# Dealing the depthwise convolution of a streaming encoder layer by channel tile: prompt tiles on POOL, VectorE and TensorE

## The chip, the cores and the metric

One core of a Trainium2 chip runs the kernel. The metric is the device time of one execution in microseconds (us); lower is better. The engines are TensorE (PE, with PEld for its weight loads), VectorE (DVE), ScalarE (ACT), GpSimd (POOL) and SyncE (SP), whose queue issues nearly all DMAs. Each engine runs its instructions strictly in the order of its own stream, and waits at an instruction whose inputs are not there.

## What is computed

The reference is one step of a two-layer streaming encoder: layer 0 is a Conformer convolution module, layer 1 is attention, and each is followed by a SwiGLU feed-forward block. The change lies in the convolution module:

```python
def conv_module(h, hist, g, w_pw1, b_pw1, w_dw, b_dw, ln_g, ln_b, w_pw2, b_pw2):
    a, gate = jnp.split(rms_norm(h, g) @ w_pw1 + b_pw1, 2, axis=-1)
    glu = a * jax.nn.sigmoid(gate)
    full = jnp.concatenate([hist.astype(glu.dtype), glu], axis=1)
    y = lax.conv_general_dilated(
        full, w_dw[:, None, :].astype(full.dtype), window_strides=(1,), padding="VALID",
        dimension_numbers=("NWC", "WIO", "NWC"), feature_group_count=D_MODEL) + b_dw
    y = jax.nn.silu(layer_norm(y, ln_g, ln_b))
    return h + y @ w_pw2 + b_pw2, full[:, -CONV_HIST:]
```

There are 1024 channels and two groups of frames: a prompt of 512 frames (one stream) and a sample group of 8 streams with 16 frames each. The depthwise convolution has 31 taps: every channel is convolved with its own 31 weights. All is float32.

## The kernel before, in words

**Layout.** Channels lie on the 128 partitions, in eight channel tiles (0 to 7). The 640 columns are 128 sample frames and then 512 prompt frames. They are cut into two column groups of 320 (`NH`): group 0 is the sample and the first 192 prompt frames, group 1 is the rest. `gall` holds the convolution's input per channel tile: `gs`, eight sample segments of 30 history and 16 new frames (368 columns), then `gp`, the prompt with its padding (544 columns).

**First projection (GLU).** `glu(c, g, ...)` (L552) computes tile c for group g: two PSUM tiles `mm` (value and gate), 24 matmuls of 320 columns each (three per k-tile, since a float32 product is made of high and low parts: L159 to L161). ACT evacuates both (L562 `t1`, L565 `t2`), and DVE multiplies them into `gall` (L569, L575). The pool `mm` has four PSUM buffers. A tile's weights come by `wsplit` (L118): a 1 MB load into `raw`, then ACT writes the rounded high part `whi` (L139) and DVE or POOL the low part `wlo` (L143). The table `PL1` says how many quarters of `wlo` POOL makes: 4 of 4 for tiles 2 to 7.

**Depthwise convolution, on DVE.** `conv` (L580) takes one or two tiles of the sample group: 31 instructions of 128x128 per tile, each multiplying a shifted window by one tap's weight and adding it to an accumulator in PSUM (L588, L591). Tiles 0 to 5 of the sample group are done so.

**Depthwise convolution, on PE.** `conv_load` (L596) lets POOL build block-diagonal weights `w4` (L598) and copies the tile's row of `gall` to a scratch `sc` in DRAM (L603). `conv_shift` (L606) reads it back in four DMAs, one per shift of 0 to 3 frames, each to 32 partitions (L609): `x4p` for the prompt, `x4s` for the sample. `conv_pe` (L613) then runs 32 matmuls of 32 output channels (L622; each shows as two in the profile), and ACT moves the result to `y` (L628). All eight prompt tiles and the sample of tiles 6 and 7 are done so. A prompt tile is one pass of 512 columns (step `p`), or is cut in 192 columns for group 0 (`A`) and 320 for group 1 (`B`).

**The rest of the module.** `conv_ln` (L631) normalizes over all 1024 channels of a group: sums over the tiles by PE with a column of 1/D (L194), spread to all partitions (L206), subtraction, squares, sums again, and silu. It needs `y` of all eight tiles. `pw2` (L651) is the second projection, with matmuls again on L159 to L161.

**What sets the order.** The string `PLAN` (L61) lists the steps: `a`, `b` are tile 0's and 1's GLU for the two groups, `cN` loads and computes the GLU of tile N, `lN` is `conv_load` and the prompt's `conv_shift`, `pN`, `AN`, `BN`, `SN` are PE convolutions (`S` is the sample group and loads its own `x4s`), `dMN` is the DVE convolution of two tiles, `n` is the norm, `w` the second projection. The tile framework's scheduler then lays every engine's stream: it keeps to the plan's order as a priority and puts a later instruction ahead where it takes an earlier one to be not ready; steps in `tc.high_priority` come sooner. On the chip the streams are fixed.

Of the kernel before, what the change touches and what calls it, by code (L numbers as in the profile page):

```python
# [8 lines left out]
F32 = mybir.dt.float32  # L9
# [6 lines left out]
P = 128  # L16
D = 1024
KT = D // P
# [23 lines left out]
HP = 2000  # L42
CUT, LCUT = 8, 6
PO = {2: 0, 4: 1}
PL1 = (0, 2, 4, 4, 4, 4, 4, 4)
PL2 = (2, 2)
SQ = 'aaaaaaaa'
C01 = 4
# [20 lines left out]
def tile_trunk(ctx, tc, xT, vecs, hist, w_pw1, w_pw2, w_in0, w_out0, w_in1, w_out1,  # L69
# [181 lines left out]
    def rms_late(g, gain, engs=SQ, cut=CUT):  # L251
        n = gr[g][1]
        xh, xl = new_xs(g)
        for k in range(KT):
            src = hp(g, k)
            if gain is not None:
                t = tp.tile([P, 384], F32, tag="n1", name=nm("n1"), bufs=NB1)
                nc.vector.tensor_scalar(out=t[:, :n], in0=src, scalar1=col(gain, k),
                                        scalar2=None, op0=ALU.mult)
                src = t[:, :n]  # L260
            xsplit(src, xh[:, k, :], xl[:, k, :])
        rt = cst.tile([P, 4], F32, tag=f"rt{g}", name=nm("rt"))
        bc, _ = rstd_bc([hp(g, k) for k in range(KT)], n, engs, cut, rt)
        b = xp.tile([P, n], F32, tag=f"bc{g}", name=nm("bc"))
        nc.scalar.activation(out=b, in_=bc, func=AF.Copy)
        return xh, xl, b, rt
# [308 lines left out]
            nc.vector.scalar_tensor_tensor(out=gp[:, c, o:o + n - ns], in0=t[:, ns:n], scalar=1.0,  # L575
                                           in1=a[:, ns:n], op0=ALU.add, op1=ALU.mult)

    def conv(cs):
        n = NB * SB
        st = w2t()  # L580
        sts = [st[:, i * 512:i * 512 + n] for i in range(len(cs))]
        for j in range(W):
            for i, c in enumerate(cs):
                src = gs[:, c, :, j:j + SB]
                dst = sts[i].rearrange("p (s w) -> p s w", w=SB)
                wj = dcol(V_DW + c * W + j)
                if j == 0:
                    nc.vector.tensor_scalar(out=dst, in0=src, scalar1=wj, scalar2=col(V_BDW, c),  # L588
                                            op0=ALU.mult, op1=ALU.add)
                else:  # L590
                    nc.vector.scalar_tensor_tensor(out=dst, in0=src, scalar=wj, in1=dst,  # L591
                                                   op0=ALU.mult, op1=ALU.add)
        for i, c in enumerate(cs):
            nc.scalar.activation(out=y[0][:, c, 0:n], in_=sts[i], func=AF.Copy)

    def conv_load(c):  # L596
        w4 = cp.tile([P, 32, 32], F32, tag="w4", name=nm("w4"), bufs=3)
# [5 lines left out]
        nc.sync.dma_start(sc, gall[:, c, :])  # L603
        return w4, sc

    def conv_shift(sc, tag, a, n, bufs):  # L606
        x4 = cp.tile([P, 4, n], F32, tag=tag, name=nm(tag), bufs=bufs)
        for s in range(4):
            nc.sync.dma_start(x4[32 * s:32 * s + 32],  # L609
                              sc[:, a + s:a + s + n].rearrange("(q p) w -> p q w", q=4))  # L610
        return x4

    def conv_pe(c, w4, x4, a, n):  # L613
        pt = mmt()
        for tg in range(8):
            for q in range(4):
                if a < 0:
                    mv = x4[:, q, :].rearrange("p (s w) -> p s w", w=SEG)
                    mv = mv[:, :, 4 * tg:4 * tg + SB]
                else:  # L620
                    mv = x4[:, q, a + 4 * tg:a + 4 * tg + n]
                nc.tensor.matmul(pt[32 * q:32 * q + 32, 0:n], w4[:, 4 * tg + q, :], mv,  # L622
                                 start=(tg == 0), stop=(tg == 7))
        o = 0 if a < 0 else NB * SB + a
        for g in range(2):
            u, v = max(o, g * NH), min(o + n, g * NH + NH)
            if u < v:
                nc.scalar.activation(out=y[g][:, c, u - g * NH:v - g * NH], in_=pt[:, u - o:v - o],  # L628
                                     func=AF.Identity, bias=col(V_BDW, c))

    def conv_ln(g):  # L631
        n = gr[g][1]
# [33 lines left out]
    zs, pws, x4s, scs = {}, {0: w00, 1: w01}, {}, {}  # L666

    def step(op, arg):
        cs = [int(c) for c in arg]
        c = cs[0] if cs else 0  # L670
        if op == "a":
            glu(c, 0, *pws[c])
        elif op == "b":
            glu(c, 1, *pws[c])
        elif op == "c":
            w = wsplit(w_pw1[c], 16, P, pool=PL1[c])
            load_hist(c, c + 1)
            glu(c, 0, *w)
            glu(c, 1, *w)
        elif op == "y":  # L680
            load_x(1)
        elif op == "x":
            xs[1] = rms(1, V_NCONV, SSQ1, 8)
        elif op == "l":
            scs[c] = conv_load(c)
            x4s[c] = conv_shift(scs[c][1], "x4p", NSC, NPC - 4, 3)
        elif op == "d":
            conv(cs)
        elif op == "S":
            conv_pe(c, scs[c][0], conv_shift(scs[c][1], "x4s", 0, NSC, 1), -1, NB * SB)  # L690
        elif op in "pAB":
            a, n = {"p": (0, T), "A": (0, NH - NB * SB), "B": (NH - NB * SB, NH)}[op]
            conv_pe(c, scs[c][0], x4s[c], a, n)
# [450 lines left out]
```

## Time and profile before

| what | value |
|---|---|
| median of three runs | 1612.81 us (1612.3 to 1614.66) |
| the profiled execution | 1610.26 us, its span 1608.3 us |
| mean granted TensorE clock over the span | 0.972 of full speed |
| PE busy over the span | 1521.2 us, 95% |
| DVE, ACT, POOL busy | 967.9 us (60%), 635.4 us (40%), 193.4 us (12%) |
| convolution stage: tile 2's GLU to the first matmul of `pw2` | from 62.60 to 241.14 us |

The profile is one execution, taken by the hardware profiler. A row of the timeline has the start, the time until the last instruction of the row ends, engine, line, operation, tiles written and read, and count; in brackets stands the idle time ahead of it and what ended that. "SPq" rows are DMA issues on SP's queue, not the transfers. A row of the windows has the busy time and count of each engine in a stretch, then the granted TensorE clock, the mean busy share of the 16 DMA engines, and GB/s. Consecutive PE instructions overlap, so a row's first instruction starts before the previous row's last has ended.

### The profile page before, as it was taken

How to read it: one execution, taken by the hardware profiler on the slowest of the kernel's cores; microseconds unless marked ns; L12 is line 12 of the kernel's file. 1: busy time of each engine (PE TensorE's matmuls, PEld its weight loads, DVE VectorE, ACT ScalarE, POOL GpSimd, SP SyncE). 2: the span in 40 equal slices, each digit the busy share in tenths (PEclk: the TensorE clock that was granted, in tenths of full speed). 3: DMA queues.
4: the chain of work that ended last, by engine and by line, in shares of the span. 5: the costliest groups of instructions: out<-in, count | busy, mean ns of one | idle time of the engine just before them, and what ended most of it. 6: DMA issues, size and time to landing. Idle time of an engine off the chain costs nothing.

```text
span 1608.3 us, 27216 instructions
## 1 busy us (share of the span) xinstructions
PE 1521.2 (95%) x11220; PEld 1426.8 (89%) x11220; DVE 967.9 (60%) x1984; ACT 635.4 (40%) x1233; POOL 193.4 (12%) x209
## 2 busy tenths in 40 slices
PE   4899789899999999999899899997999999999997
PEld 4877669889999999999888688894899999999996
DVE  7943014696566666557366766665585576666555
ACT  3312224544334244245445444454354244244243
POOL 5233303300000000002322111110100000000001
PEclk9999978899999999999999999999899999999998
DMA  6444702311312312222455445554102223213211
GB/s 216 132 131 132 196 14 79 122 36 58 111 69 76 108 62 77 99 79 79 150 175 179 165 141 170 163 172 133 65 27 79 79 80 92 88 58 105 79 54 66
DMA packets 56924, 168.78 MB, mean 105 GB/s; under 512 B 10081, under 2 KB 23009, under 8 KB 48097
## 3 DMA queue, kind: packets, MB, share of 16 engines
q1 hardware_dynamic: 56512, 166.75, 32.5%
q8 instruction: 88, 1.44, 0.4%
q10 hardware_dynamic: 288, 0.31, 0.1%
q14 instruction: 36, 0.29, 0.1%
HBM read 153.80 MB, written 13.23 MB: 104 GB/s over the span
## 4 chain that ended last, share of the span: by engine, by line
PE 89%; DVE 4%; DMA 3%; issue 2%; ACT 1%; POOL 1%; POOLq 0%; DVEq 0%; ACTq 0%; SPq 0%
PE mm L351 34%; PE mm L159 15%; PE mm L161 14%; PE mm L160 14%; PE mm L622 3%; DMA cache<-in_ck 1%; PE w L941 1%; PE am L926 1%; PE am L972 1%; PE am L909 1%; PE w L885 1%; DMA x4s<-sc 1%; PE w L886 1%; PE w L206 1%; PE w L194 1%
## 5 line engine op out<-in xcount | busy, mean ns | idle before, releaser
L351 PE MATMUL mm<-XH,wlo 128*128 128x320 f32 x736 | 229.1, 312 | 1.6 <-DVE wlo L309 1.6
L351 PE MATMUL mm<-XH,whi 128*128 128x320 f32 x736 | 227.3, 311 | 0.0
L351 PE MATMUL mm<-XL,whi 128*128 128x320 f32 x736 | 225.6, 309 | 0.0
L159 PE MATMUL mm<-xh,whi 128*128 128x320 f32 (+2 forms) x640 | 204.2, 321 | 6.2 <-ACT xh L148 5.6
L160 PE MATMUL mm<-xh,wlo 128*128 128x320 f32 (+2 forms) x640 | 203.1, 318 | 2.8 <-POOL wlo L143 2.5
L161 PE MATMUL mm<-xl,whi 128*128 128x320 f32 (+2 forms) x640 | 197.7, 316 | 0.0
L160 PE MATMUL mm<-hid,wlo 128*128 128x320 f32 (+2 forms) x560 | 171.9, 308 | 0.0
L161 PE MATMUL mm<-hid,whi 128*128 128x320 f32 (+2 forms) x560 | 169.4, 308 | 0.0
L159 PE MATMUL mm<-hid,whi 128*128 128x320 f32 (+2 forms) x560 | 167.7, 308 | 0.0
L308 ACT ACTIVATE whi<-raw 128x1536 fp32r<-128x1536 f32 (+2 forms) x90 | 101.0, 1149 | 121.7 <-PE mm L161 87.6
L309 DVE TENSOR_TENSOR wlo<-raw,whi 128x1536 fp32r<-128x1536 f32 (+2 forms) x90 | 118.7, 1341 | 40.5 <-ACT whi L308 40.4
L351 PEld LDWEIGHTS mm<-XH,wlo 128*128 128x128 f32 x736 | 139.2, 189 | 2.9 <-DVE wlo L309 2.9
L351 PEld LDWEIGHTS mm<-XH,whi 128*128 128x128 f32 x736 | 138.6, 189 | 0.0
L351 PEld LDWEIGHTS mm<-XL,whi 128*128 128x128 f32 x736 | 138.3, 189 | 0.0
L159 PEld LDWEIGHTS mm<-xh,whi 128*128 128x128 f32 x640 | 124.5, 195 | 12.3 <-ACT xh L148 6.6
L160 PEld LDWEIGHTS mm<-xh,wlo 128*128 128x128 f32 x640 | 124.8, 195 | 4.1 <-POOL wlo L143 2.7
L161 PEld LDWEIGHTS mm<-xl,whi 128*128 128x128 f32 x640 | 122.2, 193 | 1.6 <-issue 1.4
L351 PE MATMUL mm<-XH,vhi 128*128 128x320 f32 x368 | 115.0, 313 | 0.3 <-ACT XH L435 0.3
L351 PE MATMUL mm<-XL,vhi 128*128 128x320 f32 x368 | 114.5, 312 | 0.9 <-DVE XL L436 0.8
L351 PE MATMUL mm<-XH,vlo 128*128 128x320 f32 x368 | 114.8, 312 | 0.0
L160 PEld LDWEIGHTS mm<-hid,wlo 128*128 128x128 f32 x560 | 105.1, 188 | 0.0
L161 PEld LDWEIGHTS mm<-hid,whi 128*128 128x128 f32 x560 | 104.6, 188 | 0.0
(199 smaller groups left out, 3316.5 us busy)
## 6 DMA issues: line engine op xcount, KB each, us to landing
raw<-in_w_in SPq DMA_DIRECT2D x38, 1024.0 KB
cache<-in_ck SPq DMA_DIRECT2D x32, 512.0 KB
cache<-in_cv SPq DMA_DIRECT2D x32, 512.0 KB
raw<-in_w_pw SPq DMA_DIRECT2D x14, 1024.0 KB
raw<-in_w_out SPq DMA_DIRECT2D x18, 768.0 KB
x4p<-sc SPq DMA_DIRECT2D x32, 270.0 KB
raw<-in_w_kq SPq DMA_DIRECT2D x8, 1024.0 KB
raw<-in_w_in SPq DMA_DIRECT2D x12, 512.0 KB
```

Source lines behind the costliest of these rows:

```text
L159: nc.tensor.matmul(ps, wh, xh, start=(i == 0), stop=False)
L160: nc.tensor.matmul(ps, wl, xh, start=False, stop=False)
L161: nc.tensor.matmul(ps, wh, xl, start=False, stop=(i == last))
L194: nc.tensor.matmul(st[:, 512 + t * w + k:513 + t * w + k], s[:, a:a + P], onec, start=True, stop=True)
L206: nc.tensor.matmul(st[:, a:a + P], r[:, t:t + 1].to_broadcast([P, P]), ident, start=True, stop=True)
L308: nc.scalar.activation(out=hi[:, a:b], in_=src, func=AF.Copy)
L309: nc.vector.tensor_tensor(out=lo[:, a:b], in0=src, in1=hi[:, a:b].bitcast(F32), op=ALU.subtract)
L351: nc.tensor.matmul(pt, wt, v[x][:, k, :], start=(first and k == i == 0), stop=(k == 3 and i == 2), skip_group_check=True)
L622: nc.tensor.matmul(pt[32 * q:32 * q + 32, 0:n], w4[:, 4 * tg + q, :], mv, start=(tg == 0), stop=(tg == 7))
L885: nc.tensor.matmul(ps, QQ[:, q], KK[:, 0:n], start=True, stop=False)
L886: nc.tensor.matmul(ps, QQ[:, q], KL[:, 0:n], start=False, stop=True)
L909: nc.tensor.transpose(tr[:, o:o + P], S[:, SOFF[i] + k * P:SOFF[i] + (k + 1) * P], ident)
```

## The change

The plan deals the eight channel tiles otherwise. Prompt tiles 0 and 3 go to POOL (step `q`, new function `conv_pool`): for each of 31 taps ACT writes the window times the tap's weight to `cvt` (two buffers), and POOL adds it to the accumulator `ca` (30 adds of 128x512). Prompt tiles 1 and 2 go to DVE (`conv` now takes pairs of part and tile: `dp1s0` is prompt 1 with sample 0), in 31 instructions of 128x512 each, and the sample of tiles 0 to 3 stays there. Tiles 4 to 7 are on PE for both groups: `conv_shift` now loads one tile `x4` of 908 columns for both (four DMAs of 32x4x908, two buffers), and `S` reads from it. `wlo` of tiles 2 to 7 moves from POOL to DVE (`PL1`). `B6` and `B7` stand behind the step `n0` in the plan. The norm sums the tiles in another order (`LNO`), and the norm sums of `rms_late` behind the first feed-forward block get a higher priority.

```diff
-PL1 = (0, 2, 4, 4, 4, 4, 4, 4)
+PL1 = (0, 2, 0, 0, 0, 0, 0, 0)
-LNO = ((0, 1, 2, 3, 4, 5, 6, 7), (0, 1, 2, 3, 4, 5, 6, 7))
-PLAN = ("a0 y a1 x b0 b1 l0 d01 c2 l1 p0 c3 l2 p1 d23 c4 l3 p2 c5 l4 p3 d45 c6 l5 p4 c7 l6 A5 S6 l7 A6 S7 A7 s0 n0 B5 B6 B7 w0 n1 w1")
+LNO = ((0, 1, 4, 2, 5, 3, 6, 7), (0, 1, 4, 2, 5, 3, 6, 7))
+PLAN = ("a0 y a1 x b0 b1 q0 dp1s0 c2 ds1p2 c3 q3 ds2s3 c4 l4 A4 S4 B4 c5 l5 A5 S5 B5 c6 l6 A6 S6 c7 l7 A7 S7 s0 n0 B6 B7 w0 n1 w1")
...
-        bc, _ = rstd_bc([hp(g, k) for k in range(KT)], n, engs, cut, rt)
+        with tc.high_priority(offset=HP):
+            bc, _ = rstd_bc([hp(g, k) for k in range(KT)], n, engs, cut, rt)
...
+    def taps(c, part, j):
+        if part:
+            return gp[:, c, j:j + T]
+        return gs[:, c, :, j:j + SB]
+
+    def conv(items):
         st = w2t()
-        sts = [st[:, i * 512:i * 512 + n] for i in range(len(cs))]
+        sts = [st[:, i * 512:i * 512 + (T if part else NB * SB)] for i, (c, part) in enumerate(items)]
...
+    def conv_pool(c):
+        acc = cp.tile([P, T], F32, tag="ca", name=nm("ca"))
+        for j in range(W):
+            wj = dcol(V_DW + c * W + j)
+            pr = acc if j == 0 else cp.tile([P, T], F32, tag="cvt", name=nm("cvt"), bufs=2)
+            nc.scalar.activation(out=pr, in_=taps(c, 1, j), func=AF.Identity, scale=wj,
+                                 **({} if j else {"bias": col(V_BDW, c)}))
+            if j:
+                nc.gpsimd.tensor_tensor(out=acc, in0=acc, in1=pr, op=ALU.add)
+        to_y(c, NB * SB, T, acc, func=AF.Copy)
...
-    def conv_shift(sc, tag, a, n, bufs):
-        x4 = cp.tile([P, 4, n], F32, tag=tag, name=nm(tag), bufs=bufs)
+    def conv_shift(sc, n):
+        x4 = cp.tile([P, 4, NSC + NPC - 4], F32, tag="x4", name=nm("x4"), bufs=2)
         for s in range(4):
-            nc.sync.dma_start(x4[32 * s:32 * s + 32],
-                              sc[:, a + s:a + s + n].rearrange("(q p) w -> p q w", q=4))
+            nc.sync.dma_start(x4[32 * s:32 * s + 32, :, 0:n],
+                              sc[:, s:s + n].rearrange("(q p) w -> p q w", q=4))
...
-        elif op == "l":
-            scs[c] = conv_load(c)
-            x4s[c] = conv_shift(scs[c][1], "x4p", NSC, NPC - 4, 3)
+        elif op in "lm":
+            w4, sc = conv_load(c)
+            x4s[c] = w4, conv_shift(sc, NSC if op == "m" else NSC + NPC - 4)
```

What the scheduler makes of it is shown at three places. The first is PE's stream around a convolution step. Before, tile 0's convolution (line 622, input `x4p_69`) stands between the GLU of tile 2 (weights `whi_72`) and that of tile 3 (`whi_87`):

```order
L159 MATMUL mm_79_664<-xh_49_358,whi_72_577 128x320
L160 MATMUL mm_79_664<-xh_49_358,wlo_73_578 128x320
L161 MATMUL mm_79_664<-xl_50_359,whi_72_577 128x320
L622 MATMUL mm_85_703<-x4p_69_506,w4_67_502 32x512 x32
L159 MATMUL mm_89_745<-xh_16_154,whi_87_739 128x320
L160 MATMUL mm_89_745<-xh_16_154,wlo_88_740 128x320
```

Now PE's stream has tile 4's convolution (line 647, input `x4_167`, which is the shifted copy of tile 4's own GLU) right behind the GLU of tile 4 (`whi_155`) and ahead of the GLU of tile 5 (`whi_172`):

```order
L159 MATMUL mm_162_1211<-xh_49_358,whi_155_1124 128x320
L160 MATMUL mm_162_1211<-xh_49_358,wlo_156_1125 128x320
L161 MATMUL mm_162_1211<-xl_50_359,whi_155_1124 128x320
L647 MATMUL mm_168_1250<-x4_167_1245,w4_165_1241 32x192 x32
L647 MATMUL mm_169_1284<-x4_167_1245,w4_165_1241 32x128 x32
L647 MATMUL mm_170_1318<-x4_167_1245,w4_165_1241 32x320 x32
L159 MATMUL mm_174_1359<-xh_16_154,whi_172_1353 128x320
```

One GLU tile of another channel tile stood between a tile's GLU and its convolution before; none stands there now. Tiles 5, 6 and 7 have the same order (for 6 and 7 only the 192 and the 128 columns come there, and `B6`, `B7` follow behind `S7`).

The second place is SP's queue. Before, around tile 3's copies (`sc_114`, `x4p_115`) and the weights of tile 6 and 7 (`raw_133`, `raw_148`):

```order
L609 DMA x4p_99_860<-sc_98_858 32x4x540 x4
L128 DMA raw_133_1354<-in_w_pw1 128x2048
L603 DMA sc_114_1085<-gall_95 128x912
L609 DMA x4p_115_1087<-sc_114_1085 32x4x540 x4
L128 DMA raw_148_1516<-in_w_pw1 128x2048
```

Now, the same queue from tile 7's weights (`raw_204`) to tile 5's copies (`sc_183`, `x4_184`), with the first weights of `pw2` between:

```order
L128 DMA raw_204_1776<-in_w_pw1 128x2048
L627 DMA sc_166_1243<-gall_95 128x912
L633 DMA x4_167_1245<-sc_166_1243 32x4x908 x4
L128 DMA raw_246_2162<-in_w_pw2 128x2048
L627 DMA sc_183_1472<-gall_95 128x912
L633 DMA x4_184_1474<-sc_183_1472 32x4x908 x4
```

The scratch copy and the shifted loads are still one behind the other, with four instead of eight such groups, each wider by the sample's columns.

The third place is ACT's stream at the end of tile 4's GLU. Before, only the two evacuations of each half (`t2`, `t1`) and the split of the next weights stand there:

```order
L562 ACTIVATE t1_107_1022<-mm_106_997,hb1_87 128x320
L565 ACTIVATE t2_112_1080<-mm_109_1028,hb1_87 128x320
L562 ACTIVATE t1_111_1078<-mm_110_1053,hb1_87 128x320
L139 ACTIVATE whi_134_1355<-raw_133_1354 128x2048
L628 ACTIVATE y0_102<-mm_116_1092,vec_76 128x192
```

Now products for POOL (`cvt`, for prompt tile 0) stand between the evacuations of the second half of tile 4:

```order
L614 ACTIVATE cvt_93_579<-gall_95,dwv_94 128x512
L614 ACTIVATE cvt_94_582<-gall_95,dwv_94 128x512
L566 ACTIVATE t2_164_1238<-mm_161_1186,hb1_87 128x320
L614 ACTIVATE cvt_95_585<-gall_95,dwv_94 128x512
L614 ACTIVATE cvt_96_588<-gall_95,dwv_94 128x512
L563 ACTIVATE t1_163_1236<-mm_162_1211,hb1_87 128x320
L139 ACTIVATE whi_189_1582<-raw_188_1581 128x2048
```

Each `cvt` reuses the buffer of the one two before it, so it waits until POOL has added that one; the evacuation `t1` behind it waits with it.

More of the change, by code (lines that the diff above doesn't have):

```diff
@@ L576, in glu, with to_y @@
                                            in1=a[:, ns:n], op0=ALU.add, op1=ALU.mult)
-    def conv(cs):
-        n = NB * SB
+    def to_y(c, o, n, src, **kw):
+        for g in range(2):
+            u, v = max(o, g * NH), min(o + n, g * NH + NH)
+            if u < v:
+                nc.scalar.activation(out=y[g][:, c, u - g * NH:v - g * NH], in_=src[:, u - o:v - o],
+                                     **kw)
+    def taps(c, part, j):
[3 more added lines that the diff above has]
+    def conv(items):
         st = w2t()
-        sts = [st[:, i * 512:i * 512 + n] for i in range(len(cs))]
+        sts = [st[:, i * 512:i * 512 + (T if part else NB * SB)] for i, (c, part) in enumerate(items)]
         for j in range(W):
-            for i, c in enumerate(cs):
-                src = gs[:, c, :, j:j + SB]
-                dst = sts[i].rearrange("p (s w) -> p s w", w=SB)
+            for dst, (c, part) in zip(sts, items):
+                src = taps(c, part, j)
+                if not part:
+                    dst = dst.rearrange("p (s w) -> p s w", w=SB)
                 wj = dcol(V_DW + c * W + j)
@@ L592, in conv @@
                                                    op0=ALU.mult, op1=ALU.add)
-        for i, c in enumerate(cs):
-            nc.scalar.activation(out=y[0][:, c, 0:n], in_=sts[i], func=AF.Copy)
+        for dst, (c, part) in zip(sts, items):
+            to_y(c, NB * SB * part, dst.shape[-1], dst, func=AF.Copy)
+    def conv_pool(c):
[8 more added lines that the diff above has]
+        to_y(c, NB * SB, T, acc, func=AF.Copy)
     def conv_load(c):
-        w4 = cp.tile([P, 32, 32], F32, tag="w4", name=nm("w4"), bufs=3)
+        w4 = cp.tile([P, 32, 32], F32, tag="w4", name=nm("w4"), bufs=2)
         nc.gpsimd.tensor_tensor(
@@ L617, in conv_pe @@
                 if a < 0:
-                    mv = x4[:, q, :].rearrange("p (s w) -> p s w", w=SEG)
+                    mv = x4[:, q, 0:NSC].rearrange("p (s w) -> p s w", w=SEG)
                     mv = mv[:, :, 4 * tg:4 * tg + SB]
                 else:
-                    mv = x4[:, q, a + 4 * tg:a + 4 * tg + n]
+                    o = NSC + a + 4 * tg
+                    mv = x4[:, q, o:o + n]
                 nc.tensor.matmul(pt[32 * q:32 * q + 32, 0:n], w4[:, 4 * tg + q, :], mv,
                                  start=(tg == 0), stop=(tg == 7))
[L624 to L629, printed above, removed]
+        to_y(c, 0 if a < 0 else NB * SB + a, n, pt, func=AF.Identity, bias=col(V_BDW, c))
     def conv_ln(g):
@@ L664, in pw2 @@
                                                in1=hp(g, m), op0=ALU.add, op1=ALU.add)
-    zs, pws, x4s, scs = {}, {0: w00, 1: w01}, {}, {}
+    zs, pws, x4s = {}, {0: w00, 1: w01}, {}
     def step(op, arg):
-        cs = [int(c) for c in arg]
-        c = cs[0] if cs else 0
+        c = int(arg[-1]) if arg else 0
         if op == "a":
@@ L683, in step @@
             xs[1] = rms(1, V_NCONV, SSQ1, 8)
[L684 to L686 removed]
+        elif op in "lm":
+            w4, sc = conv_load(c)
+            x4s[c] = w4, conv_shift(sc, NSC if op == "m" else NSC + NPC - 4)
         elif op == "d":
[L688 removed]
+            conv([(int(arg[i + 1]), int(arg[i] == "p")) for i in range(0, len(arg), 2)])
+        elif op == "q":
+            conv_pool(c)
         elif op == "S":
[L690 removed]
+            conv_pe(c, *x4s[c], -1, NB * SB)
         elif op in "pAB":
             a, n = {"p": (0, T), "A": (0, NH - NB * SB), "B": (NH - NB * SB, NH)}[op]
[L693 removed]
+            conv_pe(c, *x4s[c], a, n)
         elif op == "s":
```

## The prediction

> **What bounds the kernel now.** I read the page's chain of waits first, then PE's timeline in the convolution stage, then windows and SP's queue there, last the prices on DVE, ACT and POOL. The chain, by engine:
>
> ```profile
> PE 89%; DVE 4%; DMA 3%; issue 2%; ACT 1%; POOL 1%; POOLq 0%; DVEq 0%; ACTq 0%; SPq 0%
> ```
>
> PE sets the end; what PE does not do or does not wait for is worth its full time. PE's timeline in the stage that the change touches:
>
> ```profile
> 62.60 0.42 PE L160 MATMUL mm<-xh,wlo 128*128 128x320 f32 x1 [2.48 <-POOL wlo L143]
> ...
> 77.82 7.07 PE L622 MATMUL mm<-x4p,w 128*32 128x512 f32 x64
> 84.83 0.41 PE L159 MATMUL mm<-xh,whi 128*128 128x320 f32 x1
> ...
> 99.10 7.07 PE L622 MATMUL mm<-x4p,w 128*32 128x512 f32 x64
> ...
> 184.22 2.81 PE L622 MATMUL mm<-x4p,w 128*32 128x192 f32 x64
> 186.85 1.93 PE L622 MATMUL mm<-x4s,w 128*32 128x128 f32 x64
> 188.59 2.78 PE L622 MATMUL mm<-x4p,w 128*32 128x192 f32 x64
> ...
> 204.93 3.64 PE L622 MATMUL mm<-x4s,w 128*32 128x128 f32 x64 [12.12 <-DMA x4s<-sc]
> 208.31 3.87 PE L622 MATMUL mm<-x4p,w 128*32 128x192 f32 x64
> ...
> 212.43 2.36 PE L622 MATMUL mm<-x4p,w 128*32 128x320 f32 x32
> ```
>
> A prompt tile costs PE 7.0 us (77.82 to 84.83), a GLU tile 14.3 (84.83 to 99.10). These alternate without a gap until tile 7's GLU ends at 184.22. The one long wait is 12.12 us at 204.93, for tile 7's own shifted copy: the only place where a tile's convolution comes soon behind its GLU. The same stage in windows, the wait and the 7.2 us behind it first:
>
> ```profile
> 192.80:204.90 12.10, 0.01 (x1) 0.00 (x1) 0.00 (x0) 0.00 (x0) 2.91 (x4) 0.53 0.89 218
> 204.90:212.10 7.20, 7.17 (x128) 6.06 (x128) 0.00 (x0) 0.37 (x1) 0.00 (x0) 0.61 0.01 2
> 62.60:77.80 15.20, 15.20 (x92) 15.03 (x92) 14.65 (x51) 2.04 (x5) 4.73 (x1) 0.89 1.04 288
> ```
>
> After the wait the granted clock is 0.61, and the same 128 instructions that took 1.93 and 2.78 take 3.64 and 3.87: a restart costs 2.8 us.
>
> **The change, part by part.** *PE's work.* Prompt tiles 0 to 3 leave PE: 4 x 7.0 = -28.0. Tile 4's prompt is cut in two (2.78 and 2 x 2.36 = 7.5 in place of 7.0): +0.5. The samples of tiles 4 and 5 come to PE: 2 x 1.93 = +3.9. Sum -23.6 us. All of it was on the path, since PE has no gap there. B5 only moves from the norm to ahead of it; B6 and B7 remain to cover the norm's sums. Two tiles (9.4 us) against three: I take no cost, and 2 us as the upper bound.
>
> *Tile 2's split.* The wait of 2.48 us at 62.60 ended with POOL's low part:
>
> ```profile
> 58.00 9.34 POOL L143 TENSOR_TENSOR wlo<-raw,whi 128x2048 fp32r<-128x2048 f32 x2 [17.13 <-ACT whi L139]
> 165.47 1.23 DVE L143 TENSOR_TENSOR wlo<-raw,whi 128x1024 fp32r<-128x1024 f32 x1 [1.31 <-ACT whi L139]
> ```
>
> POOL takes 4.67 for 2048 elements, DVE about 2 x 1.2 = 2.4: -2.3 us.
>
> *The shifted copy.* This is the large term. The new order puts the convolution of tiles 4, 5, 6 and 7 right behind the GLU of the same tile, and its first matmul needs the four loads of x4, which need the scratch copy, which needs that GLU. PE can do nothing else meanwhile, as tile 5's GLU is behind it in its stream. The chain's times, from SP's queue and the page's DMA issues:
>
> ```profile
> 100.35 0.34 SPq L603 DMA_DIRECT2D sc<-gall  x1
> 102.89 1.74 SPq L609 DMA_DIRECT2D x4p<-sc  x4
> ...
> 188.32 1.76 SPq L609 DMA_DIRECT2D x4p<-sc  x4
> 190.24 1.26 SPq L128 DMA_DIRECT2D raw<-in_w_pw  x1
> 191.60 3.79 SPq L609 DMA_DIRECT2D x4s<-sc  x4
> ...
> raw<-in_w_pw SPq DMA_DIRECT2D x14, 1024.0 KB
> x4p<-sc SPq DMA_DIRECT2D x32, 270.0 KB
> sc<-gall SPq DMA_DIRECT2D x8, 456.0 KB
> x4s<-sc SPq DMA_DIRECT2D x8, 184.0 KB
> ```
>
> GLU of tile 3 ends at 99.10; its scratch copy is issued at 100.35, the loads at 102.89: 3.79 us. Before, the next tile's GLU covered this. How long the wide loads take the trace does not show; they carry 270 + 184 = 454 KB each, 1816 KB together. The nearest row is tile 7's: from 188.32 to PE's start at 204.93, 16.6 us, the queue moved 4 x 270 + 1024 + 4 x 184 = 2840 KB, 171 KB per us with start and finish. So 1816 / 171 = 10.6 us, and a wait of 3.8 + 10.6 = 14.4 us. The lower bound is from the fastest stretch of the stage:
>
> ```profile
> 178.00:183.00 5.00, 5.00 (x36) 5.00 (x36) 0.47 (x2) 0.53 (x1) 0.00 (x0) 1.00 1.02 381
> ```
>
> At 381 GB/s the 1.86 MB take 4.9 us, with 1.6 for start and finish 6.5, so a wait of 10.3 (the 1.6 is my estimate: half of the 3.3 that the 16.6 us above leave over 2.91 MB at the waiting window's 218 GB/s). The upper bound is that the 1024 KB of weights queued behind the loads take their share of the engines: 2840 / 171 + 3.8 = 20.4. I take 14.4, since the queue is served in order and the weights are issued last. Four waits of 14.4 in place of 12.1: +45.5 us.
>
> *Restarts.* Three more restarts at a low clock, 2.8 us each: +8.4 (lower bound from the window 62.60:77.80, after a wait of 2.5 us: 15.2 in place of 14.3, so 0.9 each). The Trainium skill, page "TensorE: Matmul & The Clock Gate", section "What's actually happening", gives half rate after an idle window of about 3.4 us and full rate after about 3.4 us of work; an estimate by it is 1.7 us per restart, and the sum would be 3.3 us lower. The row is measured on these matmuls, so it stands.
>
> *POOL, DVE and ACT.* Do they hold PE up too?
>
> ```profile
> 297.56 3.76 POOL L185 TENSOR_TENSOR acc<-acc,sq 128x320 f32<-128x320 f32 x4 [0.58 <-ACT sq L166]
> 13.71 4.25 ACT L139 ACTIVATE whi<-raw 128x512 fp32r<-128x512 f32 x8
> 52.41 3.96 DVE L591 SCALAR_TENSOR_TENSOR w<-gall,dwv,w 128x128 f32<-128x128 f32 x15
> 15.14 1.29 DVE L143 TENSOR_TENSOR wlo<-raw,whi 128x512 fp32r<-128x512 f32 x2
> 59.69 3.21 DVE L575 SCALAR_TENSOR_TENSOR gall<-t,t 128x320 f32<-128x320 f32 x1
> 62.82 7.32 DVE L591 SCALAR_TENSOR_TENSOR w<-gall,dwv,w 128x128 f32<-128x128 f32 x28
> 165.51 3.43 POOL L143 TENSOR_TENSOR wlo<-raw,whi 128x1024 fp32r<-128x1024 f32 x1 [13.91 <-ACT whi L139]
> ```
>
> A POOL add of 320 columns comes every 0.94 us; with the slope of the 2048 row (4.67 - 0.94 over 1728 columns) one of 512 takes 1.35. The 59.69 row waits for POOL's first split (58.00 to 62.67), and the 165.51 row for DVE's (165.47 to 166.70): DVE instructions with two SBUF inputs and POOL's shut each other out. Up to the end of tile 4's GLU ACT must have issued 29 products, so POOL must have done 27 adds: 36.5 us, and 9.5 while DVE holds it off (three splits of 2.4 and the GLU products, some 2.3). From about 60.3, when DVE is through with tile 2's split, that is 106.3, and `t1` follows one product (0.53 us) later, at 106.8. PE is there at 60.3 + 15.2 + 2 x 14.3 = 104.1, and `t1` would start at 104.3. So the first chain is late by 2.5 us: +2.5 (bounds 0 and 8, if every DVE wait is a whole add). PE itself does not stop for it, as four PSUM buffers cover 2.5 us. DVE needs less up to there: 30 taps of 128x512 at 0.65 (the price of the split of that size), 30 of 128x128 at 0.26, splits and products 9.5, waits for POOL some 7 (eleven of half an add), in all 44 us from 61. In the waits of PE, POOL catches up: its second tile's 30 adds (41 us, from 112) fit before tile 5's chain ends at about 161. So tiles 5 to 7 get nothing added. ACT has 62 x 0.53 = 33 us more, over the stage's 180 us; it is busy 40% of the span.
>
> *The rest.* `LNO` only renames the order of sums. The higher priority in `rms_late` leaves POOL's stream in the same order there: zero.
>
> Sum: -23.6 - 2.3 + 45.5 + 8.4 + 2.5 = **+30.5 us**. The profiled execution took 1610.26 us, 1608.3 of them span; the median is 2.5 above it, well under the terms' bounds. I add to the median: 1612.8 + 30.5 = 1643.3, so **1643 us**.
>
> **Rivals.** *The loads run at the fastest rate seen.* Waits of 10.3 each: 4 x 4.1 = 16.4 less, **1627 us**. For it: longer rows per load (908 in place of 540 columns). Against it: the waiting window 192.80:204.90, in which loads of the same kind ran at 218 GB/s with the engines 89% busy. The Trainium skill, page "DMA: Bandwidth & Descriptors", "Specifications" and "Anatomy of one DMA", has line rate from 512 bytes on and 2.0 us + bytes / 436 GB/s (fitted on another path); an estimate by it is 6.3 us for the four loads, a wait of 10.1 and a sum 17 us lower. By that rule this rival; the rows with 2 KB pieces speak against it. Chance 0.12.
>
> *POOL becomes the pace.* If every add is stretched as the split at 165.51 was (3.43 in place of 2.33, half of 4.67), to 1.98 us, then 27 adds and the 9.5 end at 123.3 in place of 106.3, and the first chain starts 17 later: **1660 us**. For it: exclusion is seen. Against it: DVE's taps read PSUM as their second input, and from 62.82 on, while POOL worked until 67.3, they kept their 0.26 us each. It decides above about 1.7 us per add, where the first chain is 10 us later. Chance 0.08.
>
> *Not slower: the chain is short.* Without the waits the sum is -23.6 - 2.3 - 12.1 + 2.5 + 8.4 = -27.1 with four waits to add, so the change is no loss if a wait is under 6.8 us. The scratch copy's 3.8 alone leaves 3.0 for the loads. If bytes cost nothing, 3.8 + 1.6 = 5.4 gives -5.5, **1607 us**. For it only that no row shows the wide loads; against it that 1.86 MB in 1.4 us is over three times the best rate. Chance 0.04.
>
> *It does not do what it says:* PE's stream could have work under the waits. The order shows none for tiles 4 to 7, so this is within the 0.04.
>
> **How the numbers follow.** My forecast has 0.76, with 1643. Its own ends: 2.5 us less per wait and restarts by half give 1629; lateness 8 and waits of 16.5 give 1657. The range 1625 to 1660 takes in both rivals that are slower than before and leaves out the one that is not. No change means within 0.2% (3.2 us), about what a measurement of this kernel can tell. Of the 0.04 I put 0.03 on faster and 0.01 on same; slower has 0.96.
>
> **What would show it.** Right: PE shows four waits of 10 to 17 us ended by DMA x4<-sc, the first behind tile 4's GLU near 104 us, each followed by a stretch at a clock near 0.6; the first `pw2` matmul near 271 in place of 241 us. POOL adds near 1.35 us. Wrong: waits under 7 us; waits of PE for ACT or DVE inside the GLUs (POOL's pace); or the difference lying behind the convolution stage.

## The result and the profile after

The changed kernel takes **1639.65 us** (median; 1639.22 to 1640.6), the kernel before 1612.69 (1612.3 to 1614.66) on the same chip: ratio **1.0165, 95% interval 1.0148 to 1.0183**, so 27 us slower. The forecast was 1643 us, 1625 to 1660. The profiled execution took 1640.0 us, of which the span is 1638.2, against 1610.26 and 1608.3: +29.9 of span to account for.

The waits of the engines from 55 to 300 us of the changed kernel (engine, line, what released it: us in total, times, longest):

```profile
PE mm L647 <- DMA x<-sc: 64.5, 4, 17.5
...
ACT cvt L614 <- POOL ca L617: 33.6, 46, 2.1
```

PE waited four times for its tile's own shifted copy, and in this stretch for little else. ACT waited for POOL 46 times, but PE did not wait for ACT; ACT only made the first of the four copies late (2.8 us, below). PE's timeline shows where:

```profile
118.11 10.51 PE L647 MATMUL mm<-x,w 128*32 128x192 f32 x192 [17.54 <-DMA x<-sc]
...
157.87 11.10 PE L647 MATMUL mm<-x,w 128*32 128x192 f32 x192 [14.98 <-DMA x<-sc]
...
198.72 6.85 PE L647 MATMUL mm<-x,w 128*32 128x192 f32 x128 [14.91 <-DMA x<-sc]
...
237.43 8.94 PE L647 MATMUL mm<-x,w 128*32 128x192 f32 x162 [17.03 <-DMA x<-sc]
```

Each wait starts where the tile's GLU ended (118.11 - 17.54 = 100.57 for tile 4); at tiles 6 and 7 six short matmuls of the norm's sums, 0.7 us, stand between. What ran meanwhile, from SP's queue:

```profile
104.60 0.33 SPq L627 DMA_DIRECT2D sc<-gall  x1
107.12 1.75 SPq L633 DMA_DIRECT2D x<-sc  x4
108.97 0.47 SPq L128 DMA_DIRECT2D raw<-in_w_pw  x1
...
223.72 1.74 SPq L633 DMA_DIRECT2D x<-sc  x4
```

From GLU's end to the scratch copy's issue it is 4.0 us, to the loads' issue 2.5 more, and 11.0 from there to PE's start (13.7 at the last, 223.72 to 237.43, with the two outputs and the next weights in the queue beside it). Two of the waits, and the work behind the second, in windows (busy time of PE, PEld, DVE, ACT, POOL; then granted clock, DMA share, GB/s):

```profile
108.50:117.50 9.00, 0.00 (x0) 0.00 (x0) 9.00 (x21) 4.43 (x8) 6.47 (x6) 0.50 1.03 220
188.50:198.00 9.50, 0.00 (x0) 0.00 (x0) 0.00 (x0) 0.00 (x0) 3.29 (x4) 0.50 1.04 218
...
198.70:205.60 6.90, 6.88 (x129) 5.26 (x129) 0.00 (x0) 0.42 (x1) 0.00 (x0) 0.66 0.17 68
```

All 16 DMA engines are busy (1.03), yet only 220 GB/s move; the weights reached 381 in the window that the prediction quotes. Behind the wait PE works at a clock of 0.66 on average: 0.50 up to about 203.4, and nearly 1.00 from there.

The first `pw2` matmul stands at 277.37 in place of 241.14: +36.2, more than the span grew. The difference comes back behind it. Windows of the kernel before, tail of the stage and then the second norm:

```profile
212.10:241.10 29.00, 27.94 (x286) 18.92 (x282) 6.39 (x20) 8.54 (x17) 1.72 (x2) 0.88 0.01 1
...
241.10:300.00 58.90, 52.30 (x314) 51.84 (x315) 26.78 (x49) 27.36 (x47) 17.72 (x9) 0.83 0.22 72
```

and the same two stretches of the changed kernel:

```profile
243.90:277.40 33.50, 32.33 (x249) 26.27 (x240) 10.97 (x31) 10.78 (x22) 0.86 (x1) 0.71 0.01 1
...
277.40:330.00 52.60, 49.02 (x300) 48.65 (x301) 21.41 (x41) 25.92 (x41) 18.69 (x10) 0.86 0.24 81
```

The tail grew by 4.5 although B5 (2 x 2.36) left it; PE has nearly the same idle time there (1.2 against 1.1), but 0.71 of the clock in place of 0.88. Cut where the clock changes, first before, then now:

```profile
212.10:234.80 22.70, 22.70 (x264) 14.06 (x261) 3.61 (x10) 6.97 (x13) 0.86 (x1) 0.99 0.01 1
234.80:241.10 6.30, 5.24 (x23) 4.86 (x23) 2.79 (x10) 1.57 (x4) 0.86 (x1) 0.50 0.00 0
...
241.00:258.00 17.00, 17.00 (x252) 10.73 (x244) 3.61 (x10) 3.65 (x8) 0.00 (x0) 1.00 0.00 1
258.00:277.40 19.40, 18.23 (x88) 18.17 (x87) 7.36 (x21) 7.68 (x15) 0.86 (x1) 0.50 0.01 2
```

So the clock was back at full speed 4 us after the last wait. It fell to 0.50 soon after the last convolution had ended (at 256.8; before, at 232.4) and only the norm's short matmuls were left, with PE shown as busy nearly all the time; that stretch is 19.4 us now and was 6.3. The stretch behind the tail is 6.3 shorter: 3.3 less busy (the second group's sums were done earlier, in the tail) and 3.0 less idle.

### The profile page after: what moved, and what is told of

Its sections match the earlier page's. It is cut to its first block, busy times and chain, and to the rows that moved or that the text cites. A ratio compares the mean times of both kernels' runs of the same rounds, so it can differ in the third digit from the quotient of the medians.

```text
span 1638.2 us, 27200 instructions
## 1 busy us (share of the span) xinstructions
PE 1508.8 (92%) x11156; PEld 1435.8 (88%) x11156; DVE 996.3 (61%) x1990; ACT 675.5 (41%) x1295; POOL 244.6 (15%) x259
## 4 chain that ended last, share of the span: by engine, by line
PE 83%; DVE 5%; POOL 5%; DMA 4%; ACT 2%; issue 2%; SPq 0%; POOLq 0%; DVEq 0%; ACTq 0%
PE mm L352 34%; PE mm L159 13%; PE mm L160 13%; PE mm L161 13%; POOL ca L617 4%; PE mm L647 2%; DMA x<-sc 2%; PE w L194 1%; PE am L947 1%; PE w L962 1%; PE am L993 1%; DMA cache<-in_ck 1%; PE am L930 1%; ACT whi L139 1%; PE w L206 1%
## 5 line engine op out<-in xcount | busy, mean ns | idle before, releaser
L159 PE MATMUL mm<-xh,whi 128*128 128x320 f32 (+2 forms) x640 | 203.4, 320 | 5.0 <-ACT xh L148 4.5
```

Of the source, the lines that this page charges most:

```text
L159: nc.tensor.matmul(ps, wh, xh, start=(i == 0), stop=False)
```

## Experiments

My theory: the time lies in PE's order. PE stands in its stream behind the DRAM round trip of the very tile that it has just computed; what was dealt to POOL and VectorE costs little. Rival A: POOL's sums are the pace, and the DMA waits hide it. Rival B: the new dealing costs, whatever the order. A second question is why the loads take 11 us and not 6.5. Before was measured beside each group of runs, at 1612.49 to 1613.77 us.

**The order alone, in the kernel before.** One prompt convolution moved right behind its own GLU:

```
-... d23 c4 l3 p2 c5 l4 p3 d45 c6 l5 p4 c7 ...
+... d23 l3 c4 l4 p4 p2 c5 p3 d45 c6 l5 c7 ...
```

> The kernel before, with one prompt tile's convolution moved: p4 right behind its own GLU c4 (loads of tile 3 issued earlier, p2 and p3 later). Nothing is dealt otherwise; POOL has no sums. My theory: one wait comes in, 3.8 us of chain and 1080 KB at 171 KB per us = 6.3, so 10.1 us, and a restart of 1 to 2.8: 1612.8 + 12 = 1625 us (1621 to 1627). Rival (the new dealing to POOL and VectorE is what makes the changed kernel slower, the order alone is free): 1613 us.

Measured 1624.24 us, ratio 1.0070 (1.0047 to 1.0092). PE's row:

```profile
132.19 15.20 PE L622 MATMUL mm<-x4p,w 128*32 128x512 f32 x128 [11.17 <-DMA x4p<-sc]
```

The wait is 11.17 and the kernel 11.8 slower, with no sums on POOL. Rival B said 1613. The two numbers are not all of it: the wait that this kernel had before, for tile 7's sample copy, is 14.87 in place of 12.12, and part of both comes back behind the stage (the span of the profiled execution is 9.3 longer). One such wait of the changed kernel can be made in the old kernel without any dealing.

**One GLU tile of cover, in the changed kernel.**

```
-... c4 l4 A4 S4 B4 c5 l5 A5 S5 B5 c6 l6 A6 S6 c7 l7 A7 S7 ...
+... c4 l4 c5 l5 A4 S4 B4 c6 l6 A5 S5 B5 c7 l7 A6 S6 A7 S7 ...
```

> The changed kernel with one GLU tile put between a tile's GLU and its convolution (`c4 l4 c5 l5 A4 S4 B4 c6 l6 A5 S5 B5 c7 l7 A6 S6 A7 S7`): same work, same dealing, other order on PE. My theory (the order is what costs: PE stands behind its own tile's round trip through DRAM): a GLU tile takes PE 14.3 us, so the waits of 17.5, 15.0 and 14.9 us shrink to 3.2, 0.7 and 0.6; the last one keeps only the first four groups of tile 6 as cover, 17.0 - 4.7 = 12.3. Together 16.8 in place of 64.5, 48 us less, and some 3 us less of restarts: 1639.7 - 51 = 1589 us (1583 to 1600). Rival (POOL's sums are the pace, and the DMA waits only hide it): tile 5's last tanh stands behind 39 products, so PE would wait for ACT inside the GLUs of tiles 5 and 6, at most 10 us or so would go: 1630 us.

Measured 1590.2 us, ratio 0.9853 (0.9822 to 0.9883): 49 us less, and faster than before. PE's rows:

```profile
115.20 11.40 PE L647 MATMUL mm<-x,w 128*32 128x192 f32 x192 [3.59 <-DMA x<-sc]
...
140.80 8.86 PE L647 MATMUL mm<-x,w 128*32 128x192 f32 x192
...
163.86 4.55 PE L647 MATMUL mm<-x,w 128*32 128x192 f32 x128
...
175.09 1.44 PE L194 MATMUL w<-onec,acc 128*128 128x1 f32 x6 [6.67 <-POOL acc L185]
...
185.49 8.76 PE L647 MATMUL mm<-x,w 128*32 128x192 f32 x162 [7.67 <-DMA x<-sc]
```

Waits of 3.59, none and none in place of 17.54, 14.98 and 14.91. In the last stretch a wait for POOL's sums of the norm (6.67) stands in front of one for the copy (7.67): together 14.3, where 12.3 was expected. No GLU waits for ACT, so rival A falls here.

**Two GLU tiles of cover**, with B5 and B6 moved behind S6 (two runs of the same kernel):

```
-... c2 ds1p2 c3 q3 ds2s3 c4 l4 A4 S4 B4 c5 l5 A5 S5 B5 c6 l6 A6 S6 c7 l7 A7 S7 s0 n0 B6 B7 ...
+... c4 l4 c2 ds1p2 c5 l5 c3 q3 ds2s3 A4 S4 B4 c6 l6 A5 S5 c7 l7 A6 S6 B5 B6 A7 S7 s0 n0 B7 ...
```

> The changed kernel's dealing, ordered for cover: tile 4's and 5's GLUs come before tile 2's and 3's, so two GLU tiles lie between a GLU and its convolution; B5 and B6 are moved behind S6, to cover tile 7's round trip (`c4 l4 c2 ds1p2 c5 l5 c3 q3 ds2s3 A4 S4 B4 c6 l6 A5 S5 c7 l7 A6 S6 B5 B6 A7 S7 s0 n0 B7`). My theory: no wait at the first three tiles; the last is 17.0 - 9.4 = 7.6 us. That is 57 us less than in the changed kernel, and some 3 less of restarts: 1580 us (1573 to 1592; the upper end if the norm's sums, with B7 alone beside them, make PE wait). Rival (POOL's pace): POOL's second tile starts 14 us later, and PE or the norm waits for it: 1610 us or more.

> The same kernel as the run of 1582.2 us (0.9818 of before, 0.978 to 0.9857), with more rounds beside v6: 1582 us, 1579 to 1587.

Measured 1582.21 (0.9818, 0.978 to 0.9857) and 1583.97 us (0.9825, 0.9799 to 0.985): the lowest medians here, 1.8% under before with the changed kernel's dealing. The intervals overlap that of one GLU tile of cover. In the second run's trace the longest waits left are 3.85 us for POOL's sums and 3.96 for tile 7's copy:

```profile
176.12 1.30 PE L194 MATMUL w<-onec,acc 128*128 128x1 f32 x6 [3.85 <-POOL acc L185]
...
182.66 9.11 PE L647 MATMUL mm<-x,w 128*32 128x192 f32 x162 [3.96 <-DMA x<-sc]
```

**POOL's sums left out**, and with them ACT's products for them: of the 31 taps only the first is taken.

```
-        for j in range(W):
+        for j in range(1):
```

> The changed kernel without POOL's sums: of the 31 taps of the prompts of tiles 0 and 3 only the first is taken, so 30 products on ACT and 30 adds on POOL are left out for each; PE's, SP's and DVE's work stays. My theory (PE's waits for its own tile's round trip set the time, POOL only makes the first one late): the tanh of tile 4 comes 2.8 us earlier, the first wait falls from 17.5 to about 14.8, the other three stay: 1639.7 - 2.8 = 1637 us (1634 to 1639). Rival (POOL's sums are the pace of the stage): 60 adds of 1.46 us are gone, and the time falls by 10 us or more, to 1630 or less.

Measured 1635.86 us, ratio 1.0142 (1.0105 to 1.0179); first wait 14.68, the others 14.73, 14.54 and 16.88. All of POOL's 87.6 us of adds are worth 3.8 us, the lateness of the first chain (2.9) among them; the interval overlaps the changed kernel's (1.0148 to 1.0183), so more than that is not to be read from it. Rival A, at 10 us or more, falls a second time. A window in that wait shows the loads with ACT and POOL idle, at the same rate:

```profile
106.00:113.00 7.00, 0.00 (x0) 0.00 (x0) 7.00 (x16) 0.00 (x0) 0.00 (x0) 0.50 1.04 217
```

**The weight splits back on POOL.**

```
-PL1 = (0, 2, 0, 0, 0, 0, 0, 0)
+PL1 = (0, 2, 4, 4, 4, 4, 4, 4)
```

> The changed kernel with the weight splits of tiles 2 to 7 back on POOL where they were before, the half of each that POOL did (4.67 us). My theory: tile 2's GLU waits for POOL's half again (2.5 us, and a low clock behind it, about 4 in all), and up to the tanh of tile 4 POOL has three splits of 4.67 us more among its adds, less the 2.4 each that DVE's splits held it off: 7 us more on the first wait. Later splits fall into PE's waits. 1639.7 + 4 + 7 = 1651 us (1644 to 1657). Rival (it makes no difference who splits, for PE waits anyway): 1640 us.

Measured 1641.79 us, ratio 1.0178 (1.0144 to 1.0213): against the changed kernel's 1.0165 no difference that this can tell. My number was wrong and the rival's right. Two rows say why, PE at tile 2's GLU and ACT at tile 4's last evacuation:

```profile
57.43 0.42 PE L160 MATMUL mm<-xh,wlo 128*128 128x320 f32 x1 [0.78 <-POOL wlo L143]
```

```profile
99.38 0.53 ACT L563 ACTIVATE t<-mm,hb 128x320 f32<-128x320 f32 x1 [0.68 <-PE mm L161]
```

Tile 2 waits 0.78 for POOL's split, not 2.5, and tile 4's `t1` waited for PE and not for POOL, although POOL did four splits more up to there. But the edit moved more than the splits: the scheduler put 20 products ahead of that `t1` in ACT's stream, where the changed kernel has 29, so POOL owed fewer adds by then.

**The loads in two parts**, the prompt's columns first:

```
-x4s[c] = w4, conv_shift(sc, ... NSC + NPC - 4)
+x4s[c] = w4, conv_shift(sc, "x4p", NSC, NPC - 4), conv_shift(sc, "x4s", 0, NSC)
```

> The changed kernel with the shifted copy loaded in two: the prompt's columns (4 x 270 KB) first, the samples' (4 x 184 KB) behind them, in tiles of their own; A's matmuls need only the first four loads. If bytes set the time of the loads (11.0 us from the first issue to PE's start, for 1816 KB), the first part takes 6.5 and each of the four waits is 4.5 shorter; of that PE loses about 1 again at the first matmul of S: 4 x 3.5 = 14 less, 1626 us. If latency or the number of transfers sets it (eight in place of four), the waits stay as they are or grow: 1640 to 1650 us.

Measured 1627.56 us, ratio 1.0086 (1.0053 to 1.0119). The four waits are 51.4 us together, 13.1 less. From the first issue to PE's start:

```profile
105.13 1.75 SPq L633 DMA_DIRECT2D x4p<-sc  x4
```

```profile
112.66 4.33 PE L647 MATMUL mm<-x4p,w 128*32 128x192 f32 x64 [14.05 <-DMA x4p<-sc]
```

1080 KB took 7.53 us, 1816 KB in the changed kernel 10.99: 736 KB more for 3.46 us is 213 KB per us, and 2.5 us are left that don't depend on bytes. So it is bytes, at a low rate. The next three runs ask why the rate is low.

**Two queues**: the loads of shifts 1 and 3 on ACT's queue.

```
-            nc.sync.dma_start(x4[32 * s:32 * s + 32, :, 0:n],
+            (nc.sync, nc.scalar)[s % 2].dma_start(x4[32 * s:32 * s + 32, :, 0:n],
```

> The changed kernel with the second and fourth load of each shifted copy issued on ACT's queue in place of SP's, so that two 32-partition quarters of x4 are written at a time. In the changed kernel the loads move 220 GB/s with all 16 DMA engines busy (weights to 128 partitions reach 380 to 440). If one queue writing one quarter at a time is what halves the rate, the 11.0 to 11.8 us from first issue to PE's start fall to about 7 where ACT issues at once (tiles 6 and 7; for tiles 4 and 5 its products and copies stand ahead): 1625 to 1632 us. If the DMA engines themselves take that long per byte on this pattern, the waits of tiles 6 and 7 stay at 15 and 17 us, and the time at 1640 us or above, as ACT's loads of tile 4 come later.

Measured 1640.33 us, ratio 1.0173 (1.0135 to 1.021). For tiles 6 and 7 both queues issue within 0.1 us of each other, and the waits are 15.30 and 17.71 us, none shorter. In tile 6's:

```profile
190.00:199.50 9.50, 0.00 (x0) 0.00 (x0) 0.00 (x0) 0.00 (x0) 3.25 (x4) 0.50 1.05 221
```

**Rows of 14.6 KB**: the scratch as 32 x 4 x 912, one unbroken run per partition.

```
+        sc = dr.tile([32, 4, NSC + NPC], F32, tag="sc", name=nm("sc"), bufs=2)
+        for q in range(4):
+            nc.sync.dma_start(sc[:, q, :], gall[32 * q:32 * q + 32, c, :])
...
+            nc.sync.dma_start(x4.rearrange("p q w -> p (q w)")[32 * s:32 * s + 32, 0:m],
+                              sc.rearrange("p q w -> p (q w)")[:, s:s + m])
```

> The changed kernel with the scratch laid out as 32 x 4 x 912, so that each partition of x4 takes one unbroken run of 14.6 KB from DRAM in place of four rows of 3.6 KB; bytes, queue and the 32 partitions that a load writes stay. The scratch copy is issued in four parts in place of one (some 1.3 us more per chain). If the length of a row sets the 220 GB/s (two lengths measured so far: 3.6 KB and 2.2 KB, both about 220), the loads get nearer the weights' 380 to 440 GB/s, each wait is 4 us shorter less 1.3: 1640 - 11 = 1629 us. If it is something else (the partitions written, or reading the scratch), each wait is 1.3 longer: 1640 to 1645 us.

Measured 1641.85 us, ratio 1.0184 (1.0156 to 1.0211). Rows four times as long, the same rate:

```profile
112.00:119.00 7.00, 0.00 (x0) 0.00 (x0) 7.00 (x16) 3.14 (x5) 6.29 (x5) 0.50 0.96 210
```

**128 partitions per load**: four loads by channel quarter in place of four by shift, with partition 4p + s for channel p and shift s.

```
-        for s in range(4):
-            nc.sync.dma_start(x4[32 * s:32 * s + 32, :, 0:n],
-                              sc[:, s:s + n].rearrange("(q p) w -> p q w", q=4))
+        for q in range(4):
+            src = sc[32 * q:32 * q + 32, 0:n]
+            nc.sync.dma_start(x4[:, q, 0:n], bass.AP(tensor=src.tensor, offset=src.offset,
+                                                     ap=[[NSC + NPC, 32], [1, 4], [1, n]]))
```

> The changed kernel with the four loads of a shifted copy cut the other way: not one load per shift, which writes 32 partitions of x4, but one per quarter of the channels, which writes all 128 (partition 4p + s holds channel p shifted by s; the diagonal and the taps' weights are laid out to match). Bytes, rows of 3.6 KB, their number, the queue and the scratch stay. The Trainium skill, page "SBUF — State Buffer", section "Door 1: The DMA port swizzle (why [64,N] ≈ [32,N])", has it that a transfer to partitions 32 apart reaches the same half of the ports. Measured so far: 220 GB/s for the loads to 32 partitions, whatever the row or the queue, and 380 to 446 GB/s for transfers over 128. If the partitions that one load writes set its rate, 1816 KB at 400 take 4.6 us in place of 8.4, and each wait is 3.8 shorter: 64.5 - 15 = 49 us, 1640 - 15 = 1625 us (1621 to 1630). If the scratch, read four times over, sets it, the rate stays at 220 GB/s and the time at 1640 us.

Measured **1623.5 us**, ratio 1.0064 (1.0041 to 1.0087), against 1.0165 of the changed kernel. Windows in the loads of tiles 4, 5 and 6:

```profile
113.50:119.00 5.50, 3.29 (x10) 1.93 (x11) 5.50 (x13) 2.76 (x5) 3.21 (x3) 0.50 0.90 297
150.00:155.50 5.50, 3.45 (x10) 2.10 (x11) 5.25 (x16) 3.24 (x7) 5.19 (x5) 0.50 0.96 309
185.00:190.50 5.50, 3.18 (x11) 2.53 (x12) 0.00 (x0) 0.00 (x0) 3.45 (x4) 0.50 0.90 310
```

The windows end before the next weights, queued behind the loads, make up the traffic. The same bytes in the same rows of the same scratch now move at about 300 GB/s in place of 220. So the scratch is not the limit at 220. The run was made to test the partitions that one load writes, and they are the likely limit; but the edit also changes the order in which the rows are read (32 rows four times over in one load, in place of 128 rows once), and no run has one without the other.

The gain has two more sources that the run does not separate. Each quarter is now a load of its own, so at tiles 4 to 6 PE starts on the first one, 3.6 to 3.8 us after the issue. And the scheduler laid PE's stream otherwise: behind the first six matmuls of tile 4's convolution stand 17 of the next GLU, from here on, which cover a part of the other loads:

```profile
115.71 2.31 PE L653 MATMUL mm<-x,w 128*32 128x192 f32 x6 [11.32 <-DMA x<-sc]
117.95 0.64 PE L159 MATMUL mm<-xh,whi 128*128 128x320 f32 x1
```

The four waits are 35.5 us in place of 64.5, but the convolutions behind them last longer (2.31 us for the six matmuls above), and the kernel is 16 us faster, not 29.

**Two more orders.** First, tile 3 ahead of tile 5, so that POOL's second tile starts earlier, with the loads in two parts:

```
+... c2 ds1p2 c4 l4 c3 q3 ds2s3 c5 l5 A4 S4 B4 c6 l6 A5 S5 c7 l7 A6 S6 B5 B6 A7 S7 s0 n0 B7 ...
```

> The dealing of the changed kernel with more cover and the loads in two parts: `c2 ds1p2 c4 l4 c3 q3 ds2s3 c5 l5 A4 S4 B4 c6 l6 A5 S5 c7 l7 A6 S6 B5 B6 A7 S7 s0 n0 B7 w0 n1 w1`. Against the run in which tiles 4 and 5 went ahead of 2 and 3 (1582 us), POOL's second tile starts a GLU tile earlier, so PE's 4.5 us for POOL's sums should go, and the prompt's columns come 3.5 us before the rest, so the last wait (4.2) should nearly go: 1582 - 4.5 - 3 = 1575 us (1569 to 1583). If the norm's serial sums set the end of the stage there, neither helps: 1582.

Measured 1587.49 us (0.984, 0.9806 to 0.9873). Then, tile 3's samples on PE:

```
+... c2 ds1p2 c3 q3 m3 c4 l4 S3 ds2 c5 l5 A4 S4 B4 c6 l6 A5 S5 c7 l7 A6 S6 B5 B6 A7 S7 s0 n0 B7 ...
```

> Cover as in the run of 1582 us, but with tile 3's samples back on TensorE: 31 taps less for VectorE in the last pair, which otherwise end late, so that POOL and PE wait for them at the first norm's sums (5.7 us of PE in the run before): `c2 ds1p2 c3 q3 m3 c4 l4 S3 ds2 c5 l5 A4 S4 B4 c6 l6 A5 S5 c7 l7 A6 S6 B5 B6 A7 S7 s0 n0 B7 w0 n1 w1`. PE has 1.9 us more. If VectorE's pace sets the end of the stage, 5 less and 1.9 more: 1578 us (1573 to 1582). If the wait is for tile 7's round trip anyway, which then ends last, 1584.

Measured 1587.94 us (0.9848, 0.9823 to 0.9872). Both missed, by 12 and by 10 us. In the first, the wait for POOL's sums did not go (4.5 and 3.85 in the two runs with two GLU tiles of cover):

```profile
177.22 1.44 PE L194 MATMUL w<-onec,acc 128*128 128x1 f32 x6 [5.71 <-POOL acc L185]
```

in the second that wait is gone, and the one for tile 7's copy took its place:

```profile
185.95 8.67 PE L647 MATMUL mm<-x,w 128*32 128x192 f32 x162 [9.80 <-DMA x<-sc]
```

The second expectation's other branch (1584) came nearer. Tile 7's first matmul starts at 182.66 with two GLU tiles of cover, and at 183.74 and 185.95 in these two, each time released by its copy: in all three orders tile 7's round trip ends last there. Whether a shorter trip (128 partitions per load) would make the fastest version faster still was not tried.

## Why the prediction was right, point by point

Direction, mechanism and place were as forecast: four waits ended by the copy, the first behind tile 4's GLU, a low clock behind each. The order carries the loss: it made 11.8 us in the old kernel alone, and 49 to 57 us went from the new one with the dealing left as it is. Three of the signs were a little off: the longest wait is 17.54 (10 to 17 forecast), tile 4's GLU ends at 100.57 (104) and the first `pw2` matmul stands at 277.37 (271), the last because of the tail. The sum was 3.4 us too high against the median, and 0.6 against the profiled span (30.5 for 29.9). That it came so near is in part luck, since the terms missed in both directions, by +4.3 (the waits with the lateness), -3.5 (tile 2), -4.5 (restarts) and +2.9 (the tail, less what comes back behind it):

- **The waits.** Forecast +45.5 and +2.5 for the first chain's lateness, measured 64.46 - 12.12 = +52.3. The chain was right (3.8 forecast; 4.0 + 2.5 less the lateness of 2.8 is 3.7), the lateness too (2.8: tile 4's `t1` at 103.53, where PE ended at 100.57, less 0.2). The loads were a little under-sized: 10.6 forecast, 11.0, 11.2, 11.8 and 13.7 measured. The rate of 171 KB per us that I took included start and finish; split by the run with two parts it is 213 KB per us and 2.5 us.
- **PE's work**, -23.6. It stands in the ledger below as forecast; no run measured it apart.
- **Tile 2's split**, -2.3, failed as a reason. The wait went, and tile 4's GLU ended at 100.57 and not at the 104.1 of the prediction, which makes 5.8 us in all. But with the splits back on POOL it went as well. What both kernels share is that VectorE's taps of the first pair no longer run from 35 to 50 us (13.66 us busy before, 8.21 in both). That this is the cause is argued, not shown.
- **Restarts**, +8.4 forecast. The convolutions behind the waits last 10.5, 11.1 and 6.85 us in place of 9.4, 9.4 and 4.7 at full clock, and A7 and S7 about 1.7 more than that; less the 2.8 of before this is +3.9, 1.1 to 2.2 for one. The 1.7 by the rule of the Trainium skill that the prediction quotes (page "TensorE: Matmul & The Clock Gate", section "What's actually happening") agrees with these rows better than the 2.8 that I took from one row.
- **The tail**, for which the prediction had only B5's move, at nothing and 2 us at most. It is 9.2 us longer than its work would have it (33.5 against 29.0 less B5's 4.7). Most of it is clock: 33.5 x 0.71 = 23.8 us of full clock would take 27.0 at before's 0.88, so 6.5 by this estimate. The low clock is not left over from the wait, as it was at 1.00 from 241 to 258. The convolutions end at 256.8 with many of the norm's sums still to come, and these run at 0.50. In the run with one GLU tile of cover, with the same steps in the norm, the clock falls in the same way, after 15 us at 1.00:

```profile
190.00:205.50 15.50, 15.50 (x220) 9.36 (x209) 3.61 (x10) 3.54 (x8) 0.00 (x0) 1.00 0.01 1
206.00:225.00 19.00, 17.82 (x85) 17.77 (x85) 6.91 (x20) 7.55 (x15) 0.86 (x1) 0.50 0.01 2
```

  That B5 among these sums would have kept the clock up is argued, not shown: no run moved it alone. Behind the stage 6.3 us come back, 3.3 of work done earlier, in the tail, and 3.0 of idle time, so 2.9 us remain.

The ledger: 52.3 - 23.6 - 5.8 + 3.9 + 9.2 - 6.3 = 29.7, where the span grew by 29.9. It closes to 0.2 with PE's work as forecast.

The rivals: the loads at the fastest rate (1627) fell, since they ran at 220 GB/s. The row on which I rested (218 GB/s in a waiting window) was the right one, but I read it as the effect of the 2 KB pieces, and the runs with 14.6 KB rows and with 128 partitions show that it was not the pieces. The Trainium skill, page "SBUF — State Buffer", section "Door 1: The DMA port swizzle (why [64,N] ≈ [32,N])", states this: a transfer to 32 partitions reaches 8 of 16 ports, 218 GB/s at most. The traces agree within a few per cent, with 210 to 225. By the same page's section "Can I just issue two DMAs to hit both halves?" two transfers don't add up, and the run on two queues agrees with 221. It is a weak test of that, since the two loads then under way write neighbouring blocks of 32 partitions and not the two halves. Had I set this page against the rule of 436 GB/s that I quoted from the Trainium skill's page "DMA: Bandwidth & Descriptors", an estimate by it, 1816 KB at 218 and 2 us, is 10.5 us for the loads, where 11.0 to 13.7 were measured. POOL as the pace (1660) fell in three runs (one and two GLU tiles of cover, and POOL's sums left out). A short chain (1607) fell with the waits.

## What to carry to other kernels

In an in-order engine, put between a producer and a consumer that meet through DRAM at least as much other work of that engine as the round trip takes, here one to two GLU tiles for 15 to 17.5 us. Dealing work away from the bound engine gains only what the order lets it gain: the same dealing was 1.7% slower or 1.8% faster than before. And look at how many partitions one transfer writes before asking about its rows or its queue.

## What the runs showed of the hardware that was not expected

- Loads that write 32 partitions each ran at 210 to 225 GB/s with the DMA engines shown as fully busy, with rows of 2.2, 3.6 or 14.6 KB, from one queue or two, with POOL and ACT busy or idle; the same bytes written over 128 partitions, and read in another order, ran at 297 to 310.
- A busy share of 1.03 of the DMA engines thus said nothing about their rate; the GB/s column did.
- After a wait of 15 to 17.5 us the granted clock was 0.50 for the next 3 to 5 us of work (to 121.4, 162.4, 203.4 and 240.9 in the changed kernel) and about 1.00 from there.
- With PE shown as busy for 18.23 of 19.40 us, and no idle time over 1.2 us, the granted clock was still 0.50 (258.00 to 277.40), where PE's work was the norm's short matmuls of one column and of 128.
- POOL's add of 128x512 took 1.46 us on average (60 in 87.6 us; the median is 1.30), and ACT's product of that size 0.72, where I had 1.35 and 0.53:

```profile
L617 POOL TENSOR_TENSOR ca<-ca,cvt 128x512 f32<-128x512 f32 x60 | 87.6, 1460 | 28.0 <-ACT cvt L614 21.9 <-ACT ca L614 2.2
L614 ACT ACTIVATE cvt<-gall,dwv 128x512 f32<-128x512 f32 x60 | 42.8, 721 | 33.6 <-POOL ca L617 33.6
```
